# Sixteen DRAM-to-DRAM DMAs of one hybrid-mixer kernel get a fixed place in GpSimd's order

## The chip, the cores and the metric

One core of a Trainium2 chip runs the whole program in one launch. The metric is the device time of one execution in microseconds (us); lower is better. The core has TensorE (PE, with its weight loads as PEld), VectorE (DVE), ScalarE (ACT), GpSimd (POOL) and SyncE (SP), each with its own instruction order, and 16 DMA engines. All queues share those 16 engines. SP's and ACT's DMAs run on hardware queues, GpSimd's on the software queue q0.

## The reference

One layer, 512 tokens, width 2048, float32:

```python
mod = c_act @ w_ada + b_ada;  shift, scale, gate = split(mod, 3)
h = rmsnorm(x, norm_pre) * (1 + scale) + shift
q_a, f_a, v_a, z_a, v_b, z_b, g_a, g_b = split(h @ w_in, ...)
o_a = hgrn2_mixer(q_a, f_a, v_a, lb)                  # 8 heads, chunks of 64
y_a = o_a / rms(o_a) * hgrn_norm * silu(z_a)
y_b = pool_mixer(v_b, pool_w, pool_scale) * silu(z_b)
merged = sigmoid(g_a) * (y_a @ w_proj_a) + sigmoid(g_b) * (y_b @ w_proj_b)
out = merged @ w_out
x + gate * rmsnorm(out, norm_post)
```

## The kernel before

Every large product keeps float32 accuracy by splitting both operands in a high and a low part and running three matmuls. So each weight piece is loaded raw by SP (tile `..._raw`), copied to `..._hi` by ACT, and its `..._lo` is the difference, made by DVE or GpSimd. Rings of four buffers each hold the raw, the hi and the lo pieces (lines 173 to 176).

The stages, in order of time:

- **Start.** SP loads `x` (16 loads), then the rows of `w_ada` (tiles `ada`, 128 loads of 256 KB; each is 256 runs of 1 KB), mixed with pieces `A_raw`, `B_raw`, `C_raw` of `w_in` (24 loads of 512 KB, 256 runs of 2 KB each). ACT squares `x` for the norm (`junk`), DVE sums `ada` rows into `ada_acc` and `ada_sum`, `make_h` (line 295) turns a pair of row sums into two of the 16 tiles of `h` (`h_hi`, `h_lo`), and PE multiplies each piece of `w_in` with them (tile `g`). In this stage GpSimd makes `A_lo`, `B_lo`, `C_lo` and all `h_lo` (lines 317 and 653), tied in one chain by `then("POOL", ...)`. A table of planned times sets the order. The stage ends where PE begins `v_ps`.
- **Heads and pooling.** The products `q`, `v`, `vb`, `zb`, `za`; the eight heads of `hgrn` run in slices between their matmuls. `finish_a(h)` (line 572) stores a head's result to DRAM (`ya_dram`) from GpSimd's queue.
- **Gates g.** Sixteen steps (line 859) for two output tiles each. A step loads four pieces `g_raw` (512 KB, 512 runs of 1 KB each), and eleven of them also load six rows of the gate's weights, `gw` (256 KB, 128 runs of 2 KB each), which DVE sums into `gate` (lines 621 and 623). SP issues all loads in one order (`load`, line 70), each behind the one before. PE has 96 matmuls per step.
- **Projections pa, pb**, from `y` tiles which GpSimd loads back (line 891), and then the **output** product by one level of Strassen's scheme. Its B operands are sums and differences of quarters of `w_out`; four of them per half of the columns (`wsum`, eight DRAM tiles of 2 MB) are made beforehand by DMA alone.

Those sums are the matter here: 16 DMAs of 2 MB on GpSimd's queue (lines 845 to 855 list them, line 881 issues them, two per step). Eight copy a quarter of `w_out` into a `wsum` tile, four add a second quarter of `w_out`, and four add another `wsum` tile. An adding DMA waits for the copy below it and for the tile that it reads. They depend on nothing else, and the program's scheduler is free to put them anywhere in GpSimd's order that their place in the code allows. In the kernel before it has put them first. The first readers are the `wo_raw` loads of the output stage.

Of the kernel before, what the change touches and what calls it, by code (L numbers as in the profile page):

```python
# [34 lines left out]
def trunk(ctx, tc, x, c, w_ada, b_ada, norm_pre, norm_post, w_in, lower_bounds, hgrn_norm,  # L35
          pool_w, pool_scale, w_proj_a, w_proj_b, w_out, out):
    nc = tc.nc
# [15 lines left out]
    def t_s(name, dt=F32):  # L53
        return act.tile([P, S], dt, tag="s", bufs=32, name=name)

    def t_w(name, n=S, dt=F32):
        return act.tile([P, 544], dt, tag="w", bufs=10, name=name)[:, :n]
# [7 lines left out]
    def t_pg(name):  # L65
        return pg.tile([P, S], F32, tag="pg", name=name)

    last_load = [None]

    def load(dst, src):  # L70

# [10 lines left out]
    def ins_of(d):  # L82
        return getattr(d, "ins", d)
# [38 lines left out]
    def finish_heads(n):  # L122
        while steps and len(heads_done) < n:
            tick(1)
# [211 lines left out]
    def in2(name, c0):  # L336
        outs = [t_ps(f"{name}_ps0"), t_ps(f"{name}_ps1")]
        proj2(name, w_in, KT, c0, hh, hl, outs)
        return outs
# [31 lines left out]
    y_dram = [dram.tile([NH, P, S], F32, name="ya_dram"), dram.tile([NH, P, S], F32, name="yb_dram")]  # L371
# [195 lines left out]
    def gate_a(h, p):  # L567
        sz = t_w(f"sza_{h}")
        nc.scalar.activation(sz, p, AF.Silu)
        sz_a[h] = sz  # L570

    def finish_a(h):
        y = o_sb[h]
        nc.vector.scalar_tensor_tensor(y, y, vec[:, R_HN + h:R_HN + h + 1], sz_a[h], op0=ALU.mult, op1=ALU.mult)
        nc.gpsimd.dma_start(y_dram[0][h], y)

    pooled = [None] * NH

# [35 lines left out]
    def gate_rows(j, k):  # L614

        if k == 0:
            gate[j] = t_w(f"gate_{j}")
        t = t_w(f"gw_{j}_{k}")
        load(t, w_ada[k * P:(k + 1) * P, 2 * D + j * S:2 * D + (j + 1) * S])
        if k == 0:  # L620
            nc.vector.tensor_scalar(gate[j], t, c_act[:, 0:1], None, op0=ALU.mult)
        else:
            nc.vector.scalar_tensor_tensor(gate[j], t, c_act[:, k:k + 1], gate[j], op0=ALU.mult, op1=ALU.add)  # L623

    def gate_finish(j):

        acc = gate[j]
        br = t_w(f"bg_{j}")
        load(br[0:1, :], b_ada[:, 2 * D + j * S:2 * D + (j + 1) * S])
        nc.vector.tensor_add(acc[0:1, :], acc[0:1, :], br[0:1, :])  # L630
        np_b = t_w(f"npost_{j}")
        load(np_b, norm_post[:, j * S:(j + 1) * S].to_broadcast([P, S]))
        gp = t_pg(f"gate_ps_{j}")
        hi, lo = split(f"gate_{j}", acc, lambda name, dt: t_w(name, S, dt))
        matmul(gp, ones_v, hi, True, False)
        matmul(gp, ones_v, lo, False, True)
        nc.vector.scalar_tensor_tensor(acc, gp, float(P), np_b, op0=ALU.mult, op1=ALU.mult)
# [220 lines left out]
    for b, off in ((0, OFF_GA), (1, OFF_GB)):  # L858
        for m in range(0, KT, 2):
            if (b, m) == (0, ZA_AT):  # L860
                for h in range(0, NH, 2):
                    o2 = in2(f"za{h}", OFF_ZA + h * P)
                    gate_a(h, o2[0]); gate_a(h + 1, o2[1])
                    if h < 6:
                        finish_heads(h + 2)
                        finish_a(h); finish_a(h + 1)
            o2 = in2(f"g{b}_{m}", off + m * P)
            if (b, m) == (0, ZA_AT + 2):
                finish_heads(NH)
                finish_a(6); finish_a(7)  # L870

            first = ZA_AT // 2 + 2
            step = b * KT // 2 + m // 2 - first
            for i in range(max(0, step * GATE_PER), min(4 * KT, (step + 1) * GATE_PER)):
                gate_rows(i // KT, i % KT)
                if i % KT == KT - 1:
                    gate_finish(i // KT)
            if b * KT + m >= 8 and wsum_steps:
                for _ in range(2):
                    dst, src, kw = wsum_steps.pop(0)  # L880
                    nc.gpsimd.dma_start(dst, src, **kw)
            for r in range(2):
                sig[b][m + r] = t_s(f"sig{b}_{m + r}")
                nc.scalar.activation(sig[b][m + r], o2[r], AF.Sigmoid)
# [3 lines left out]
    for b in range(2):  # L888
        for k in range(NH):
            y = t_w(f"y{b}_{k}")  # L890
# [213 lines left out]
```

## Time and profile before

| | us |
|---|---|
| median of 3 runs | 1494.02 (1493.1 to 1494.7) |
| the profiled execution | 1494.7 |
| its span, first to last instruction | 1493.0 |
| PE busy | 1325.5 (89%) |
| DVE, ACT, POOL busy | 815.3, 561.0, 246.3 |
| DMA moved | 238.11 MB |

The profiled execution is 1.7 us longer than its span. The page of the profile gives totals and the chain of work that ended last. The view by stretches gives each engine's busy time, the clock that PE was granted (1.00 is 2.4 GHz, 0.50 is 1.2 GHz), the share of time the 16 DMA engines were busy, and the rate. Views in order of time show single instructions with the idle time before them and what ended it.

### The profile page before, as it was taken

How to read it: one execution, taken by the hardware profiler on the slowest of the kernel's cores; microseconds unless marked ns; L12 is line 12 of the kernel's file. 1: busy time of each engine (PE TensorE's matmuls, PEld its weight loads, DVE VectorE, ACT ScalarE, POOL GpSimd, SP SyncE). 2: the span in 40 equal slices, each digit the busy share in tenths (PEclk: the TensorE clock that was granted, in tenths of full speed). 3: DMA queues.
4: the chain of work that ended last, by engine and by line, in shares of the span. 5: the costliest groups of instructions: out<-in, count | busy, mean ns of one | idle time of the engine just before them, and what ended most of it. 6: DMA issues, size and time to landing. Idle time of an engine off the chain costs nothing.

```text
span 1493.0 us, 16400 instructions
## 1 busy us (share of the span) xinstructions
PE 1325.5 (89%) x6031; PEld 1088.9 (73%) x6031; DVE 815.3 (55%) x1336; ACT 561.0 (38%) x787; POOL 246.3 (16%) x269
## 2 busy tenths in 40 slices
PE   0230499999999999999999999999999999999996
PEld 0010377788888888887888888888888888887885
DVE  0211259754345967868768434434425455578667
ACT  3010153443353554554555422222224222245552
POOL 3100264521222232232223000000001000000010
PEclk9975699999999999999999999999999999999998
DMA  9999988933222223223233445554634333335576
GB/s 307 294 284 231 266 293 287 305 99 99 85 71 92 71 92 106 71 92 113 72 127 100 141 156 175 186 169 152 198 120 160 101 93 98 99 127 189 192 244 221
DMA packets 170232, 238.11 MB, mean 159 GB/s; under 512 B 8780, under 2 KB 120484, under 8 KB 169128
## 3 DMA queue, kind: packets, MB, share of 16 engines
q1 hardware_dynamic: 155528, 188.78, 39.4%
q0 software_dynamic: 13312, 46.14, 11.3%
q10 hardware_dynamic: 1312, 2.14, 0.4%
q8 instruction: 47, 0.77, 0.2%
q14 instruction: 33, 0.27, 0.1%
HBM read 228.64 MB, written 41.94 MB: 181 GB/s over the span
## 4 chain that ended last, share of the span: by engine, by line
PE 79%; DVE 6%; issue 4%; DMA 1%; POOL 1%; ACT 1%; DVEq 0%; ACTq 0%; POOLq 0%
PE g_ps L91 23%; PE out L91 7%; PE vb_ps L91 6%; PE za_ps L91 6%; PE v_ps L91 6%; PE pb L91 6%; PE pa L91 6%; PE g L91 5%; PE zb_ps L91 5%; PE q_ps L91 3%; PE lv L91 2%; DVE ada_acc L105 1%; PE o L91 1%; DMA ada<-in_w_ada_dram 1%; PE mix L91 1%
## 5 line engine op out<-in xcount | busy, mean ns | idle before, releaser
L91 PE MATMUL g_ps<-h_hi,g_hi 128*128 128x512 f32 x512 | 200.1, 391 | 0.0
L91 PE MATMUL g_ps<-h_hi,g_lo 128*128 128x512 f32 x512 | 199.4, 389 | 0.0
L91 PE MATMUL g_ps<-h_lo,g_hi 128*128 128x512 f32 x512 | 199.3, 389 | 0.0
L177 ACT CAST g_hi<-g_raw 128x1024 fp32r<-128x1024 f32 x64 | 67.3, 1053 | 196.3 <-PE g_ps L91 161.0
L178 DVE TENSOR_TENSOR g_lo<-g_raw,g_hi 128x1024 fp32r<-128x1024 f32 x61 | 74.5, 1222 | 108.7 <-ACT g_hi L177 107.4
L105 DVE SCALAR_TENSOR_TENSOR ada_acc<-ada,c_act,ada_acc 128x512 f32<-128x512 f32 x104 | 74.3, 751 | 92.0 <-DMA ada<-in_w_ada_dram 91.8
L91 PEld LDWEIGHTS g_ps<-h_hi,g_lo 128*128 128x128 f32 x512 | 96.1, 188 | 20.1
L91 PEld LDWEIGHTS g_ps<-h_hi,g_hi 128*128 128x128 f32 x512 | 96.1, 188 | 20.0
L91 PEld LDWEIGHTS g_ps<-h_lo,g_hi 128*128 128x128 f32 x512 | 96.1, 188 | 19.9
L178 DVE TENSOR_TENSOR wo_lo<-wo_raw,wo_hi 128x1024 fp32r<-128x1024 f32 x56 | 68.3, 1223 | 43.8 <-ACT wo_hi L177 43.8
L177 ACT CAST wo_hi<-wo_raw 128x1024 fp32r<-128x1024 f32 x56 | 59.0, 1054 | 68.2 <-PE out L91 52.9
L91 PE MATMUL g<-h_hi,A_lo 128*128 128x512 f32 x64 | 26.2, 409 | 64.9 <-POOL A_lo L105 64.9
L623 DVE SCALAR_TENSOR_TENSOR gate<-gw,c_act,gate 128x512 f32<-128x512 f32 x60 | 45.0, 751 | 44.9 <-DMA gw<-in_w_ada_dram 43.7
L91 PEld LDWEIGHTS g<-h_hi,A_lo 128*128 128x128 f32 x64 | 12.5, 196 | 68.1 <-POOL A_lo L105 65.4
L1039 POOL DMA_DIRECT2D xr<-in_x_dram x16 | 8.7, 548 | 306.2 <-PE out L91 306.2
L891 POOL DMA_DIRECT2D y<-ya_dram x8 | 4.4, 550 | 288.3 <-DMA npost<-in_norm_post_dram 231.2
L91 PE MATMUL vb_ps<-h_hi,vb_hi 128*128 128x512 f32 x128 | 51.5, 402 | 0.0
L91 PE MATMUL za_ps<-h_hi,za_hi 128*128 128x512 f32 x128 | 51.1, 399 | 0.0
L91 PE MATMUL out<-wo_lo,op_hi 128*128 128x512 f32 x128 | 49.9, 390 | 1.3 <-DVE wo_lo L178 1.3
L91 PE MATMUL zb_ps<-h_hi,zb_hi 128*128 128x512 f32 x128 | 50.9, 398 | 0.0
L91 PE MATMUL v_ps<-v_hi,h_hi 128*128 128x512 f32 x128 | 50.5, 394 | 0.0
L91 PE MATMUL vb_ps<-h_hi,vb_lo 128*128 128x512 f32 x128 | 50.1, 391 | 0.0
(343 smaller groups left out, 3394.0 us busy)
## 6 DMA issues: line engine op xcount, KB each, us to landing
ada<-in_w_ada_dram SPq DMA_DIRECT2D x128, 256.0 KB, 6.6
g_raw<-in_w_in_dram SPq DMA_DIRECT2D x64, 512.0 KB, 3.6
wsum<-in_w_out_dram POOLq DMA_DIRECT2D x12, 2048.0 KB, 40.0
gw<-in_w_ada_dram SPq DMA_DIRECT2D x64, 256.0 KB, 4.8
wo_raw<-wsum SPq DMA_DIRECT2D x32, 512.0 KB, 4.1
wo_raw<-in_w_out_dram SPq DMA_DIRECT2D x24, 512.0 KB, 4.1
wsum<-wsum POOLq DMA_DIRECT2D x4, 2048.0 KB, 37.0
v_raw<-in_w_in_dram SPq DMA_DIRECT2D x16, 512.0 KB, 3.7
```

What stands on the lines that cost most here:

```text
L91: d = nc.tensor.matmul(o, lhsT, rhs, start=start, stop=stop, skip_group_check=onto)
L105: d = f(*args, **kw)
L177: last_w[0] = ins_of(nc.scalar.copy(hi, raw))
L178: (eng or (nc.gpsimd if steps and next(turn) else nc.vector)).tensor_sub(lo, raw, hi.bitcast(F32))
L623: nc.vector.scalar_tensor_tensor(gate[j], t, c_act[:, k:k + 1], gate[j], op0=ALU.mult, op1=ALU.add)
L891: nc.gpsimd.dma_start(y, y_dram[b][k])
L1039: nc.gpsimd.dma_start(xr[t][j], x[t * P:(t + 1) * P, j * S:(j + 1) * S])
```

## The change

The 16 DMAs are issued behind the last GpSimd DMA that `finish_a` issued, and each behind the one before. `tc.issue_after` fixes an order on the engine. It adds no wait for a transfer to land.

```diff
-    last_load = [None]
+    last_load, last_pool = [None], [None]
...
     def finish_a(h):
         y = o_sb[h]
         nc.vector.scalar_tensor_tensor(y, y, vec[:, R_HN + h:R_HN + h + 1], sz_a[h], op0=ALU.mult, op1=ALU.mult)
-        nc.gpsimd.dma_start(y_dram[0][h], y)
+        last_pool[0] = ins_of(nc.gpsimd.dma_start(y_dram[0][h], y))
...
                 for _ in range(2):
                     dst, src, kw = wsum_steps.pop(0)
-                    nc.gpsimd.dma_start(dst, src, **kw)
+                    with tc.issue_after(last_pool[0]):
+                        last_pool[0] = ins_of(nc.gpsimd.dma_start(dst, src, **kw))
```

GpSimd's order at the program's start, before: the masks' last instructions, the sums (tiles `wsum_0` belong to the first half of the columns, `wsum_1` to the second), and the first difference that PE needs.

```order
L881 DMA wsum_0_4757<-wsum_0_4756 256x2048
L881 DMA wsum_1_4762<-in_w_out_dram 1024x512
L881 DMA wsum_1_4760<-wsum_1_4759 256x2048
L881 DMA wsum_1_4761<-wsum_1_4760 256x2048
L105 TENSOR_TENSOR A_lo<-A_raw,A_hi 128x1024
L105 TENSOR_TENSOR h_lo<-hf_349,h_hi 128x512
```

The same place after:

```order
L160 COPY mask_pair<-mask_pair_133 128x64
L160 COPY mask_pair<-mask_pair_138 128x64
L105 TENSOR_TENSOR A_lo<-A_raw,A_hi 128x1024
L105 TENSOR_TENSOR h_lo<-hf_349,h_hi 128x512
L105 TENSOR_TENSOR B_lo<-B_raw,B_hi 128x1024
```

All 16 sums have left the place ahead of `A_lo`; nothing but the masks stands there now.

GpSimd's order where they stand after the change, from the store of the last two heads (`ya_dram`) to the first reload of a head's result (`y_0`):

```order
L575 DMA ya_dram<-o_5386 128x512
L575 DMA ya_dram<-o_5843 128x512
L882 DMA wsum_0_4755<-in_w_out_dram 1024x512
L882 DMA wsum_0_4756<-in_w_out_dram 1024x512
L882 DMA wsum_0_4757<-in_w_out_dram 1024x512
L882 DMA wsum_0_4758<-in_w_out_dram 1024x512
L882 DMA wsum_0_4755<-in_w_out_dram 1024x512
L882 DMA wsum_0_4756<-wsum_0_4755 256x2048
L882 DMA wsum_0_4757<-wsum_0_4756 256x2048
L882 DMA wsum_0_4758<-in_w_out_dram 1024x512
```

Eight more rows of the same kind follow for `wsum_1`, and then the loads of `y`, which before stood directly behind the two stores. The order of PE, DVE, ACT and SP is the same as before but for line numbers.

## Rows read from the trace of the kernel before

**Rows 1.** The page: busy time per engine, then the chain that ended last.

```profile
PE 1325.5 (89%) x6031; PEld 1088.9 (73%) x6031; DVE 815.3 (55%) x1336; ACT 561.0 (38%) x787; POOL 246.3 (16%) x269
...
PE 79%; DVE 6%; issue 4%; DMA 1%; POOL 1%; ACT 1%; DVEq 0%; ACTq 0%; POOLq 0%
```

**Rows 2.** Stretches: length, busy us (instructions) per engine, PE's clock, DMA share, GB/s.

```profile
0.00:170.00 170.00, 25.16 (x40) 9.77 (x40) 26.66 (x48) 19.27 (x49) 25.45 (x68) 0.77 1.03 277
170.00:330.00 160.00, 153.39 (x706) 125.17 (x707) 104.33 (x155) 72.73 (x115) 75.23 (x40) 0.97 0.79 255
...
844.00:1152.00 308.00, 308.00 (x1360) 254.96 (x1359) 130.22 (x147) 85.56 (x104) 8.78 (x16) 1.00 0.52 170
```

**Rows 3.** Waits, 0 to 330 us: who waited for whom, total us, times, longest.

```profile
PE g L91 <- POOL A_lo L105: 64.9, 1, 64.9
```

**Rows 4.** POOL in order of time: start, us, instruction, idle before and releaser.

```profile
7.00 0.94 POOL L881 DMA_DIRECT2D wsum<-in_w_out_dram  x1
...
49.14 1.33 POOL L881 DMA_DIRECT2D wsum<-in_w_out_dram  x1 [22.11 <-DMA wsum<-in_w_out_dram]
...
166.85 0.88 POOL L881 DMA_DIRECT2D wsum<-wsum  x1 [34.69 <-DMA ada<-in_w_ada_dram]
167.43 2.67 POOL L105 TENSOR_TENSOR A_lo<-A_raw,A_hi 128x1024 fp32r<-128x1024 f32 x1
```

**Rows 5.** SP's issues in order of time, 0 to 175 us.

```profile
12.92 56.89 SPq L76 DMA_DIRECT2D ada<-in_w_ada_dram  x16
...
115.28 3.38 SPq L76 DMA_DIRECT2D C_raw<-in_w_in_dram  x1
118.71 40.60 SPq L76 DMA_DIRECT2D ada<-in_w_ada_dram  x8
...
170.13 0.37 SPq L76 DMA_DIRECT2D A_raw<-in_w_in_dram  x1
```

**Rows 6.** Stretches again, just after the last of the sums.

```profile
185.00:195.00 10.00, 9.91 (x56) 8.34 (x55) 4.76 (x7) 6.26 (x13) 4.43 (x3) 1.00 1.06 355
```

**Rows 7.** All engines in order of time, from the start to the released matmul.

```profile
9.48 0.61 ACT L268 ACTIVATE junk<-x 128x512 f32<-128x512 f32 x1
...
90.91 0.75 DVE L105 SCALAR_TENSOR_TENSOR ada_sum<-ada,c_act,ada_acc 128x512 f32<-128x512 f32 x1 [2.70 <-DMA ada<-in_w_ada_dram]
...
102.13 1.04 ACT L105 CAST A_hi<-A_raw 128x1024 fp32r<-128x1024 f32 x1 [48.35 <-DMA A_raw<-in_w_in_dram]
...
103.61 0.78 ACT L105 ACTIVATE h_hi<-xT,sh,g 128x512 fp32r<-128x512 f32 x1
...
170.16 0.80 PE L91 MATMUL g<-h_hi,A_lo 128*128 128x512 f32 x1 [64.92 <-POOL A_lo L105]
```

**Rows 8.** The chain that ended last, in order of time: start, us, what.

```profile
329.62 43.52 PE v_ps L91 x192
...
834.57 97.97 PE g_ps L91 x432
```

**Rows 9.** POOL: the last head's store and the first reload.

```profile
843.20 0.54 POOL L575 DMA_DIRECT2D ya_dram<-o  x1 [18.86 <-DVE o L574]
1074.96 0.55 POOL L891 DMA_DIRECT2D y<-ya_dram  x1 [231.21 <-DMA npost<-in_norm_post_dram]
```

**Rows 10.** SP and DVE in order of time, one step of the gates.

```profile
1001.11 2.88 SPq L76 DMA_DIRECT2D gw<-in_w_ada_dram  x6
...
1006.93 16.20 SPq L76 DMA_DIRECT2D g_raw<-in_w_in_dram  x4
...
1007.16 3.90 DVE L623 SCALAR_TENSOR_TENSOR gate<-gw,c_act,gate 128x512 f32<-128x512 f32 x5 [0.25 <-DMA gw<-in_w_ada_dram]
```

**Rows 11.** Waits of ACT and of SP's queue, 844 to 1152 us.

```profile
ACT g_hi L177 <- PE g_ps L91: 154.3, 45, 4.4
...
SPq L76 <- DVE g_lo L178: 210.7, 48, 6.0
```

**Rows 12.** The page's DMA queues: packets, megabytes, share of 16 engines' span.

```profile
q0 software_dynamic: 13312, 46.14, 11.3%
```

## The prediction

> **What bounds the kernel now.** I read the page first: PE is busy for 1325.5 us of 1493.0 and makes 79% of the chain that ended last [rows 1]. The view by stretches shows where it is not the bound: in the stretches shown from 170 us on PE hardly stops, but of the first 170 us it works 25 [rows 2]. There the waits name one thing: PE waits 64.9 us, once, for GpSimd's `A_lo` [rows 3]. GpSimd is not busy either. Its order in time shows the sums standing ahead of `A_lo`: the first is issued at 7.00 us, some of them wait for earlier ones to land (22.11 us at one place, 34.69 at the last), the last goes at 166.85, and `A_lo` follows at 167.43 [rows 4], though `A_hi` had been made at 102.13 [rows 7]. So the first fault is GpSimd's order. The second is in SP's order: while the sums run, its loads crawl. Sixteen `ada` loads take 56.89 us, 3.56 each, and eight later ones 40.60, 5.1 each [rows 5]. When the sums are over, the DMA engines move 355 GB/s of SP's loads alone [rows 6], 0.74 us per 256 KB. In 0 to 170 us the DMA share is already 1.03 [rows 2]: that stage is bound by DMA, and the sums are most of it.
>
> **The start, without the sums.** The 16 loads of `x` and 16 of `ada` are 32 times 0.74 us, some 24 us, issued from 1.3 us on; with 2 us to land, the last row is there at about 28. ACT squares 16 blocks of `x` from 9.48 us at 0.61 each [rows 7], to 19.3; the norm takes some 3 us of short steps, and DVE, whose order puts 11 of the 16 sums behind it, adds them at 0.75 each until about 31. From the last sum to the first matmul there lie the shift and scale, `A_hi` (1.04) and `h_hi` (0.78) [rows 7], some 4 us, and beside them `A_lo` at 2.67 [rows 4]. The matmul that was released at 170.16 [rows 7] goes at about 35. That is 135 us earlier; bounds 125 (rows landing at two thirds of that rate) and 138.
>
> From there to `v_ps` at 329.62 [rows 8] it took 159.5 us, of which PE was busy 153.4 [rows 2], the first microseconds at a lower clock (mean 0.77 over the stretch before, against 0.97). Can the stage hold this pace when it begins without the rows that the blocked kernel had already fetched? 112 `ada` loads and 22 pieces remain, 29.4 and 11.5 MB, at 355 GB/s 115 us, less than PE needs; DVE has 104.3 us of work there and some more sums, still less. I take 155 us, 4 less than before, bounds 150 to 166. **The start gains 139 us, bounds 128 to 143.** Everything between, up to the last head's store, shifts along with PE, whose order there is not touched.
>
> **The new place.** The last store goes out at 843.20 [rows 9] (I keep the clock of before for places). GpSimd then has nothing to do until it reloads `y` at 1074.96 [rows 9], 231 us later: a wait of GpSimd inside the sums holds up no one but those reloads, and the sums' issues cost nobody anything. What they bring along is the other thing: their load on the DMA engines. PE works the gates without a pause until 1152, with a DMA share of 0.52 and 170 GB/s [rows 2].
>
> How do SP's loads fare beside the sums? From 12.92 to 170.13 us SP issued 41 loads (37 `ada` and four pieces, the first and last in [rows 5]), each of 256 runs: 157.2 / 41 = 3.83 us per 256 runs. It goes by runs, not by bytes: a `C_raw` of 512 KB in 256 runs of 2 KB took SP 3.38 us, an `ada` of 256 KB in 256 runs of 1 KB 3.56 [rows 5]. A step of the gates loads four `g_raw` of 512 runs and six `gw` of 128: 2816 runs, 11 times 256, 42.1 us beside the sums. PE's 96 matmuls of the step take 97.97 / 432 * 96 = 21.8 us [rows 8]. **Beside the sums PE gets fed at 0.52 of its pace.**
>
> How long? Before, the sums lasted from 7.00 us to about 182 (the last is issued at 166.85 [rows 4], and from 185 on SP's loads have the full rate [rows 6]): 175 us. I take the same. In it PE gets food for 175 * 0.52 = 91 us; 84 are missing.
>
> What is loaded ahead pays for a part. ACT's `g_hi` waits for PE, 45 times in this stretch, and SP for DVE's `g_lo`, 48 times [rows 11]: the rings are full, four raw pieces and three split ones ahead, 7 * 5.44 = 38 us. But DVE's order also has the sums of `gw`: those that SP issues at 1001.11 are added from 1007.16 on [rows 10], and the next `g_lo` stands behind them. A late `gw` stops DVE while later `g_raw` lie there, so only the three split pieces count, 16 us. Loss: 84 - 16 = 68; with what a lower clock after PE's pauses costs, 69. Bounds: 47, if all 38 us count, to 95, if none counts and the pauses cost 10 of clock.
>
> One bound comes from another row. q0 had 11.3% of the engines' time, 169 us [rows 12]; 48 of its transfers are the 256 KB ones of `y`, `x` and the stores, at 0.74 us each 36 us, so the sums alone are worth 134 us of all 16 engines. If they lasted only that long, the loss would be 134 * 0.48 - 16 = 48.
>
> The Trainium skill ("DMA: Bandwidth & Descriptors", Anatomy of one DMA) gives 2.0 us plus the bytes over 436 GB/s for a DMA of GpSimd's queue: as an estimate by that page 6.8 us for 2 MB, 109 us for all 16, and a loss of 109 * 0.48 - 16 = 36 in place of 68. The trace speaks against it: 175 us for the same 16 beside SP's loads, 134 without them.
>
> Behind the gates nothing changes: the first reader of `wsum` is a load of the output stage, behind all the projections.
>
> **The sum.** 1494.7 (profiled execution) - 139 + 69 = 1425. The median of three is 0.7 lower than that execution, so I leave it at 1425.
>
> **The rivals.**
>
> - *Short sums:* without the exposed waits of the start they run at their own 134 us or less (by the page just named 109), loss 36 to 48: 1392 to 1404. For it: q0's share. Against: SP's loads run beside them at either place. 0.13.
> - *Hidden:* the engines have 0.48 of 308 us free, 148 us, which holds the sums' 134, and the rings cover the rest: loss 0 to 15, 1356 to 1371. Against: SP's pace in [rows 5] is what a queue gets beside the sums, not what it asks for. 0.08.
> - *A new wait at the start:* DVE's sums or late `ada` rows take `A_lo`'s place, and the gain there is about 100 us: 1455 to 1470. For it: the stage then needs DVE for over 110 of 155 us, and its rows just in time. 0.08.
> - *Slower:* SP's queue asks more at the new place than at the start, and the sums take twice as long, 350 us: the loss is 350 * 0.48 - 16 = 152, and the reloads of `y` go late too: 1508. It decides from 320 us of duration on, where the loss passes the 139 gained. For it: four of the sums wait for the one before with nothing between them. 0.04.
> - *It doesn't do what it says:* GpSimd still waits ahead of `A_lo`. The order of the instructions leaves no sum there. 0.02, 1494.
>
> **How the numbers follow.** My forecast, 1404 to 1455, has 0.65. The range of 8 in 10 reaches to the upper part of the short sums and into the weak start: 1393 to 1462. A measurement of this kernel can tell some 0.2%, 3 us, from no change. Faster 0.94, same 0.02, slower 0.04.
>
> **What the profile after would show.** Right: PE's long wait for `A_lo` gone and `v_ps` starting at 185 to 200 us; 355 GB/s from the start on; the last store of a head 139 us earlier; behind it, for 160 to 195 us, PE with pauses that DVE's `g_lo` and behind it DMAs of `gw` end, 69 us in total; no pause from there on. Wrong: `v_ps` after 210 us (the start has another bound), PE without pauses in the gates (the sums are hidden), or pauses that reach into the projections.

## The result and the profile after

The changed kernel takes 1423.28 us (median, 1418.05 to 1425.48) beside 1494.36 for the kernel before: a ratio of 0.952, 95% interval 0.9491 to 0.9549. The forecast was 1425. The profiled execution took 1424.94 us, its span 1423.2, 69.8 less than the span before.

The page of the changed kernel, answering to [rows 1] and [rows 12]: busy times, the chain that ended last by engine, the software queue.

```profile
PE 1328.0 (93%) x6031; PEld 1091.8 (77%) x6031; DVE 812.6 (57%) x1336; ACT 559.2 (39%) x787; POOL 246.3 (17%) x269
...
q0 software_dynamic: 13312, 46.14, 12.0%
...
PE 76%; DMA 14%; DVE 7%; issue 1%; SPq 1%; ACT 1%; POOL 0%; DVEq 0%; ACTq 0%
```

The work is the same; DMA now has 14% of the chain, where it had 1%. GpSimd in order of time, answering to [rows 4] and [rows 9]: the first difference, the last head's store, the sums, the first reload.

```profile
32.39 2.37 POOL L105 TENSOR_TENSOR A_lo<-A_raw,A_hi 128x1024 fp32r<-128x1024 f32 x1 [23.74 <-ACT A_hi L105]
...
706.40 0.54 POOL L575 DMA_DIRECT2D ya_dram<-o  x1 [18.86 <-DVE o L574]
706.93 3.05 POOL L882 DMA_DIRECT2D wsum<-in_w_out_dram  x4
...
813.97 1.34 POOL L882 DMA_DIRECT2D wsum<-in_w_out_dram  x1 [35.05 <-DMA wsum<-in_w_out_dram]
...
866.55 1.62 POOL L882 DMA_DIRECT2D wsum<-in_w_out_dram  x1
1005.34 0.61 POOL L892 DMA_DIRECT2D y<-ya_dram  x1 [137.18 <-DMA npost<-in_norm_post_dram]
```

`A_lo` is made at 32.39 us in place of 167.43, right behind `A_hi`; the matmul that it releases starts at 34.81 (before 170.16). GpSimd's long waits are now in the sums, where nobody waits for it. The chain in order of time, with the start of `v_ps` ([rows 8] has 329.62 for it), and pieces of it from the gates:

```profile
192.82 43.52 PE v_ps L91 x192
...
738.80 5.29 PE g_ps L91 x22
...
774.59 21.50 DMA gw<-in_w_ada_dram
796.86 1.23 DVE g_lo L178
798.13 12.49 PE g_ps L91 x46
...
812.87 29.82 DMA gw<-in_w_ada_dram
...
843.45 1.23 DVE g_lo L178
844.70 6.92 DMA g_raw<-in_w_in_dram
...
887.78 40.81 PE g_ps L91 x166
```

On this chain single loads of `gw` take 15 to 30 us. The waits of PE and of DVE behind the last store (total us, times, longest):

```profile
PE g_ps L91 <- DVE g_lo L178: 53.5, 8, 22.3
...
DVE gate L623 <- DMA gw<-in_w_ada_dram: 150.7, 29, 30.9
```

And the stretches, with the columns of [rows 2]: the start, the heads, the gates beside the sums, and the gates behind them.

```profile
35.00:190.00 155.00, 148.43 (x692) 120.99 (x692) 111.99 (x165) 71.45 (x114) 74.94 (x39) 0.98 0.85 277
193.00:706.00 513.00, 511.11 (x2485) 428.12 (x2484) 342.47 (x686) 254.54 (x348) 127.69 (x130) 1.00 0.29 91
706.00:892.00 186.00, 132.53 (x530) 105.94 (x530) 47.73 (x55) 28.52 (x34) 15.49 (x17) 0.85 1.02 277
...
912.00:1082.00 170.00, 170.00 (x752) 140.70 (x751) 71.97 (x81) 50.85 (x63) 8.86 (x16) 1.00 0.54 172
```

The table takes three marks from each trace: the start of `v_ps`, the last head's store (`ya`), and the first matmul of `pa`. The heads' column is the time from the first mark to the second, the gates' column from the second to the third. The loss in the gates is against the 308.8 us of the kernel before. Copies first, all in the start, no `gw`, `gw` not read and the first short runs were executed once each, so their times have no interval; the other times are medians.

| kernel | time | `v_ps` | `ya` | `pa` | heads | gates | loss in the gates |
|---|---|---|---|---|---|---|---|
| before | 1494 | 329.5 | 843.2 | 1152.0 | 513.7 | 308.8 | 0 |
| changed | 1423.3 | 192.7 | 706.4 | 1082.2 | 513.7 | 375.8 | 67.0 |
| copies first | 1441.2 | 243.0 | 756.7 | 1098.4 | 513.7 | 341.7 | 32.9 |
| all in the start, spaced | 1470.3 | 303.4 | 818.7 | 1127.5 | 515.3 | 308.8 | 0 |
| no `gw` | 1380.7 | 194.9 | 708.6 | 1038.7 | 513.7 | 330.1 | 21.3 |
| `gw` loaded, not read | 1409.9 | 192.2 | 706.0 | 1067.1 | 513.8 | 361.1 | 52.3 |
| short runs | 1414.1 | 194.1 | 707.8 | 1071.4 | 513.7 | 363.6 | 54.8 |
| spaced in the gates | 1384.3 | 193.5 | 707.3 | 1042.6 | 513.8 | 335.3 | 26.5 |
| the same, short runs | 1385.2 | 192.0 | 705.8 | 1040.4 | 513.8 | 334.6 | 25.8 |
| spread over the heads | 1365.3 | 191.3 | 712.5 | 1021.3 | 521.2 | 308.8 | 0 |
| the same, short runs | 1366.1 | 189.0 | 714.0 | 1022.7 | 525.0 | 308.7 | 0 |
| copies close, adds apart | 1361.6 | 191.3 | 711.3 | 1020.1 | 520.0 | 308.8 | 0 |
| copies in a block, in the heads | 1362.6 | 193.0 | 709.6 | 1018.3 | 516.6 | 308.7 | 0 |

Start -136.8, gates +67.0: net 69.8, the difference of the two spans.

### The profile page after: what moved, and what is told of

Read it like the earlier page. It is cut to its first block, busy times and chain, and to the rows that moved or that the text cites. A ratio compares the mean times of both kernels' runs of the same rounds, so it can differ in the third digit from the quotient of the medians.

```text
span 1423.2 us, 16399 instructions
## 1 busy us (share of the span) xinstructions
PE 1328.0 (93%) x6031; PEld 1091.8 (77%) x6031; DVE 812.6 (57%) x1336; ACT 559.2 (39%) x787; POOL 246.3 (17%) x269
## 3 DMA queue, kind: packets, MB, share of 16 engines
q0 software_dynamic: 13312, 46.14, 12.0%
## 4 chain that ended last, share of the span: by engine, by line
PE 76%; DMA 14%; DVE 7%; issue 1%; SPq 1%; ACT 1%; POOL 0%; DVEq 0%; ACTq 0%
PE g_ps L91 18%; PE out L91 8%; DMA gw<-in_w_ada_dram 8%; PE vb_ps L91 6%; PE za_ps L91 6%; PE v_ps L91 6%; PE pb L91 6%; PE pa L91 6%; PE g L91 5%; PE zb_ps L91 5%; DMA ada<-in_w_ada_dram 4%; PE q_ps L91 3%; PE lv L91 2%; DMA g_raw<-in_w_in_dram 1%; SPq L76 1%
## 5 line engine op out<-in xcount | busy, mean ns | idle before, releaser
L91 PE MATMUL g_ps<-h_hi,g_lo 128*128 128x512 f32 x512 | 205.3, 401 | 53.5 <-DVE g_lo L178 53.5
L91 PE MATMUL g_ps<-h_hi,g_hi 128*128 128x512 f32 x512 | 204.5, 399 | 0.0
L91 PE MATMUL g_ps<-h_lo,g_hi 128*128 128x512 f32 x512 | 203.2, 397 | 0.0
L91 PEld LDWEIGHTS g_ps<-h_hi,g_hi 128*128 128x128 f32 x512 | 99.0, 193 | 20.6
L91 PE MATMUL za_ps<-h_hi,za_lo 128*128 128x512 f32 x128 | 50.0, 391 | 0.0
L91 PE MATMUL vb_ps<-h_lo,vb_hi 128*128 128x512 f32 x128 | 50.0, 390 | 0.0
L91 PE MATMUL zb_ps<-h_hi,zb_lo 128*128 128x512 f32 x128 | 49.9, 390 | 0.0
```

The source lines that it names most:

```text
L91: d = nc.tensor.matmul(o, lhsT, rhs, start=start, stop=stop, skip_group_check=onto)
```

## The experiments

Two theories stood against each other for each half of the change. At the start: did GpSimd's blocked order make it late, or the sums' load on the DMA engines? In the gates: what makes PE wait there, and could it be avoided? The cuts of the edits show where a sum is issued; where the building of the list of sums moves with it, that part is left out.

**Copies first.** The eight copies go back to the program's start, the eight adds stay behind the last store.

```diff
-                    with tc.issue_after(last_pool[0]):
-                        last_pool[0] = ins_of(nc.gpsimd.dma_start(dst, src, **kw))
+                    if kw:
+                        with tc.issue_after(last_pool[0]):
+                            last_pool[0] = ins_of(nc.gpsimd.dma_start(dst, src, **kw))
+                    else:
+                        nc.gpsimd.dma_start(dst, src)
```

> The eight copies go back to the program's start, ahead of A_lo; the eight adding DMAs stay behind the last head's store. Copies wait for nothing, so GpSimd is free for A_lo at about 15 us. Theory (shared DMA engines): the start is late by the DMA load alone. The copies last some 80 to 90 us there, 32 loads of x and ada take as long, and v_ps starts at 240 to 265 us in place of 192.8. The adds alone last some 115 us beside the gates and cost 30 to 40 us there in place of 67. Together 1445 to 1465 us. Rival (GpSimd's order): only the waits on GpSimd ahead of A_lo cost time at the start; v_ps starts at 195 to 200 us, and the total is 1390 to 1400 us.

Measured 1441.2 us; `v_ps` at 243.0, loss in the gates 32.9. The copies wait for nothing, so GpSimd was not blocked: ahead of `A_lo` it waits for ACT's `A_hi`.

```profile
81.45 2.35 POOL L105 TENSOR_TENSOR A_lo<-A_raw,A_hi 128x1024 fp32r<-128x1024 f32 x1 [66.59 <-ACT A_hi L105]
```

And yet the start came 50 us later than in the changed kernel, so the rival falls. The total lies 4 us below the range given, since start and loss both came out in the lower halves of theirs.

**All sums in the start, none that waits ahead of the first difference.** The copies at the program's start, the adds one by one in GpSimd's chain of the start stage.

```diff
         chains[engine] = ins_of(d)
+        if engine == "POOL":
+            pieces[0] += 1
+            if pieces[0] >= ADDS_FROM and pieces[0] % 3 == 0 and wsum_list:
+                dst, src2, kw = wsum_list.pop(0)
+                with tc.issue_after(chains[engine]):
+                    chains[engine] = ins_of(nc.gpsimd.dma_start(dst, src2, **kw))
```

> All 16 sums at the start again, but not as a block ahead of GpSimd's first difference: the eight copies at the program's start, the eight adds one by one between GpSimd's differences of the start stage, every third one from the twelfth on. Theory A (the sums' load on the DMA engines made the start late, GpSimd's order only put that in one place): first matmul of g at 80 to 90 us as with the copies alone, v_ps at 295 to 325, nearly as late as before the change, no loss in the gates, total 1458 to 1490. Theory B (GpSimd's blocked order made it late): v_ps at 240 to 255 as with the copies alone, total 1403 to 1420.

Measured 1470.3 us, `v_ps` at 303.4. Waits of GpSimd, ACT and DVE in its first 303 us (total us, times, longest), and the stretch itself:

```profile
POOL A_lo L107 <- ACT A_hi L107: 103.5, 4, 67.4
...
ACT A_hi L107 <- DMA A_raw<-in_w_in_dram: 73.1, 5, 27.4
...
DVE ada_acc L107 <- DMA ada<-in_w_ada_dram: 117.0, 32, 25.7
...
0.00:303.00 303.00, 184.20 (x742) 139.97 (x743) 131.25 (x201) 91.20 (x163) 99.94 (x106) 0.90 0.99 289
```

Now it is GpSimd that waits for ACT, and ACT and DVE for SP's loads; none of GpSimd's waits there is for a sum, and the DMA engines are busy for 0.99 of the time. Theory A holds: with the order mended and the sums still in the stage, `v_ps` comes 26 us earlier than before the change; the other 111 us come only when the sums leave the stage.

**What the late `gw` cost.** First 60 of the 64 `gw` loads with their sums are left out of the changed kernel, then the loads stay and only 60 of DVE's sums are left out.

```diff
+        if k > 0:
+            return
```

```diff
-        else:
-            nc.vector.scalar_tensor_tensor(gate[j], t, c_act[:, k:k + 1], gate[j], op0=ALU.mult, op1=ALU.add)
```

> The changed kernel with 60 of the 64 rows of the gate's weights left out, their loads and their sums on DVE (the gate vector is then incomplete). Theory (SP's loads are late by runs, and the late gw rows stop DVE ahead of g_lo): a step needs 2048 runs, 30.7 us beside the sums against 21.8 of PE, and with no gw sum in DVE's order all the 38 us of pieces ahead count: the loss in the gates falls from 67 us to 0 to 15, total 1358 to 1373. Rival (the sums disturb something else: PE's clock, GpSimd and DVE on one port, memory as such): the pauses stay, above 1400.

> The changed kernel with the same gw loads, but 60 of the 64 sums on DVE that read them are left out (the gate vector is then incomplete). SP's queue has the same runs to move; only DVE no longer waits for gw ahead of g_lo. Theory: the missing food is the same 84 us, but 38 us of pieces ahead count in place of 16, so the loss is 45 to 55 in place of 67: total 1403 to 1413. Rival a (all of the loss is DVE's wait for gw): total 1358 to 1370. Rival b (the pieces ahead play no part): 1425.

Measured 1380.7 us, 8 above the theory's range, and 1409.9, within it. PE's waits behind the last store, without `gw` (the first two lines) and then with `gw` not read:

```profile
PE g_ps L91 <- DVE g_lo L178: 8.7, 5, 6.6
PE g_ps L91 <- ACT g_hi L177: 4.7, 3, 1.9
```

```profile
PE g_ps L91 <- ACT g_hi L177: 25.9, 5, 13.9
PE g_ps L91 <- DVE g_lo L178: 12.1, 5, 6.7
```

So of the 67.0 us, 15 go when DVE's order no longer stops at a late `gw`, as expected (45 to 55 left). That kernel also spares DVE 60 sums and SP its waits until DVE has read a `gw`, 11.4 us in the changed kernel; no run takes these apart. Another 31 go with the loads of `gw`. The 21 that are left without `gw` are more than the 0 to 15 expected: 13.4 us of waits, and the rest is matmuls that took longer. PE did 719 matmuls in 170.62 busy us of this stretch at a granted clock of 0.96:

```profile
708.00:892.00 184.00, 170.62 (x719) 137.50 (x718) 37.18 (x36) 36.09 (x44) 15.49 (x17) 0.96 1.01 263
```

At [rows 8]'s 97.97 / 432 = 0.227 us each they are worth 163.1, so 7.5 us are slower matmuls.

**Short runs.** All sums are asked for in runs of 1 KB; the copies and the adds from `w_out` and from `wsum` had 2, 2 and 8 KB.

```diff
-            wsum_steps += [(dst, first, {}), (dst, second, {"accum_op": ALU.add, "max_dma_last_dim": 8192})]
+            wsum_steps += [(dst, first, {"max_dma_last_dim": 1024}), (dst, second, {"accum_op": ALU.add, "max_dma_last_dim": 1024})]
```

> The changed kernel with all 16 sums cut in runs of 1 KB, copies too; same place, same bytes. Theory (the DMA engines take turns by runs, so a short run of the sums holds SP's next one up for less time): SP gets more food per us beside the sums, the sums last 215 to 330 us, the loss in the gates, from the last head's store to the first projection, falls from 67 to 20 to 50 us, total 1378 to 1408. If only the adds are cut in the end, the loss is 30 to 45. Rival (the engines share by bytes or by time, whatever the size of a run): the loss stays at 60 to 75, total 1418 to 1432.

Measured 1414.1 us, loss 54.8: between the two theories. The queue's packets tell that only the adds were cut (13312 before, 11264 more now, which is what the eight adds make at 1 KB):

```profile
q0 software_dynamic: 24576, 46.14, 13.5%
```

Something is gained, less than by the theory of turns. Both halves of that theory's account are seen: in 186 us behind the last store SP issued 24 pieces `g_raw` and 36 `gw` in place of 21 and 31, and the last sum (issued at 902.36 us, 38.3 us to landing) was there at 940.7 us in place of 897.2, so the sums stood beside SP's loads for longer.

```profile
g_raw<-in_w_in_dram SPq DMA_DIRECT2D x24, 512.0 KB, 11.8
...
gw<-in_w_ada_dram SPq DMA_DIRECT2D x36, 256.0 KB, 17.0
...
902.36 4.67 POOL L882 DMA_DIRECT2D wsum<-in_w_out_dram  x1
```

**Spread over the heads.** Each second difference that GpSimd makes in the heads' stage is followed by one sum, copies first, then the adds of the two halves in turn.

```diff
-        (eng or (nc.gpsimd if steps and next(turn) else nc.vector)).tensor_sub(lo, raw, hi.bitcast(F32))
+        e = eng or (nc.gpsimd if steps and next(turn) else nc.vector)
+        d = ins_of(e.tensor_sub(lo, raw, hi.bitcast(F32)))
+        if e is nc.gpsimd and wsum_list:
+            pieces[0] += 1
+            if pieces[0] % SUM_EVERY == 0:
+                dst, src2, kw = wsum_list.pop(0)
+                with tc.issue_after(d):
+                    nc.gpsimd.dma_start(dst, src2, **kw)
```

> The sums are issued one at a time between GpSimd's lo pieces of the heads and pooling stage, some 22 us apart, the eight copies first and then the adds of the two halves in turn. Theory: a sum of 2 MB lasts 10 to 14 us beside SP's loads, the stage's loads then run at half pace for that long and at full pace for the rest of the 22 us, and 38 us of pieces ahead cover it: no loss anywhere, the start stays at 192.8 us and the gates go without a pause: 1355 to 1365 us. Rival (the same DMA work costs PE the same wherever it lies beside its loads): about 1425. A second rival: an adding DMA's wait on GpSimd holds up the lo pieces behind it, 1370 to 1400.

Measured 1365.3 us (1360.82 to 1370.14), a ratio of 0.9142 (0.9111 to 0.9173) to the kernel before, 0.3 us above the theory's range: the gates lose nothing, the heads 7.5 us, where no loss was expected.

**The same with short runs of the adds, and with the adds further apart.** The second has the copies behind every difference and the adds behind every third.

```diff
-            if pieces[0] % SUM_EVERY == 0:
+            if len(wsum_list) > 8 or pieces[0] % SUM_EVERY == 0:
```

> The kernel with the sums spread over the heads' stage, its eight adds cut in runs of 1 KB in place of 8 KB. Theory (turns by runs; the two pauses of PE near 469 and 558 us stand beside adds with 8 KB runs): the pauses beside the adds go, v_ps to the last head's store takes 513 to 517 us in place of 521, total 1356 to 1363. Rival (the pauses come from the bytes): 521 us again, total 1361 to 1370.

> The same spread, 8 KB runs kept, the copies behind every difference of GpSimd and the adds behind every third. Theory (the pauses come from adds that are issued 16 to 25 us apart and each last about as long): with 30 to 40 us between adds the pauses go, total 1356 to 1363. Rival (copies at 10 to 14 us apart now starve SP in the v stage): new pauses between 230 and 340 us, total 1366 to 1385.

With short runs 1366.1 us (0.9153, 0.9131 to 0.9176), heads 525.0 us: no gain, so the theory of turns falls here as a forecast. The adds themselves took longer, 22.4 and 21.6 us (median, from `w_out` and from `wsum`) in place of 19.3 and 15.1. With the adds apart 1361.6 us (0.9108, 0.9093 to 0.9124), inside its range. Its interval and that of the first spread overlap a little, and the heads' stage took 520.0 us in place of 521.2: crowding the copies did no harm, but that the distance of the adds brings a gain isn't shown.

**Is it the place or the spacing?** The spread kernels changed both. So one kernel spaces the sums within the gates (GpSimd splits every third piece of `g` and issues a sum behind it), and one puts the copies as a block into the heads' stage (the adds apart as above).

```diff
-        e = eng or (nc.gpsimd if steps and next(turn) else nc.vector)
+        pieces[0] += gates[0]
+        e = eng or (nc.gpsimd if (steps and next(turn)) or (gates[0] and wsum_list and pieces[0] % SUM_EVERY == 1) else nc.vector)
```

```diff
-                dst, src2, kw = wsum_list.pop(0)
+                for _ in range(8 if len(wsum_list) > 8 else 1):
+                    dst, src2, kw = wsum_list.pop(0)
```

> The sums stay in the gates' stage, where the change put them, but are issued one at a time: every third piece of g is split by GpSimd in place of VectorE, and one sum follows it, some 16 us apart; copies first, adds of the two halves in turn. Theory (a row of sums without gaps starves SP; with gaps SP catches up at its full pace): while a sum runs (12 us) SP loads 3.1 of the 256-run units, in the 4.4 us of gap another 5.9, together 9.0 where PE needs 8.3, so the loss from the last head's store to the first projection is 0 to 20 us, total 1357 to 1378. Rival (the place decides: the gates' own loads leave too little of the DMA engines, however the sums are spaced): loss 40 to 70, total 1397 to 1430.

> The eight copies in one block at the first difference of GpSimd in the heads' stage, the eight adds behind every third difference. Theory (what counts is what the stage asks of SP: there one piece of 512 runs in some 6 us and no gw rows, against 7.7 us for it beside the sums, so 0.78 of PE's pace; a block of 85 us misses 19 us, and the rings hold 38): the block is hidden, v_ps to the last head's store takes 513 to 519 us, total 1356 to 1364. Rival (a block costs wherever it stands, as the eight copies cost 50 us at the start): 20 to 40 us lost there, total 1378 to 1400.

The block in the heads is hidden: 1362.6 us (0.9121, 0.9107 to 0.9134), heads 516.6 us, theory held. Its stretch with the block, from 190 to 300 us, has PE busy throughout beside a DMA share of 0.75:

```profile
190.00:300.00 110.00, 110.00 (x517) 91.79 (x516) 48.27 (x99) 48.90 (x63) 26.66 (x26) 1.00 0.75 246
```

Spaced in the gates the sums cost 26.5 us, 1384.3 in all (0.927, 0.9239 to 0.9301): between the theory's range and the rival's. Its GpSimd also takes 16 differences out of DVE's order, where a late `gw` would hold them up, so not all of what is gained on the block need be the spacing; no run takes the two apart. Its two stretches, first the copies, then the adds:

```profile
706.00:846.00 140.00, 139.98 (x617) 115.57 (x616) 58.94 (x60) 34.89 (x42) 25.59 (x17) 1.00 0.82 270
846.00:1042.00 196.00, 177.26 (x750) 145.01 (x749) 65.67 (x73) 49.66 (x63) 36.20 (x32) 0.94 0.94 244
```

And the DMA issues from 846 us on (KB each, median us to landing), after a line for the copies before that:

```profile
wsum<-in_w_out_dram POOLq DMA_DIRECT2D x8, 2048.0 KB, 12.6
```

```profile
wsum<-in_w_out_dram POOLq DMA_DIRECT2D x4, 2048.0 KB, 20.8
wsum<-wsum POOLq DMA_DIRECT2D x4, 2048.0 KB, 15.4
```

Copies of 12.6 us, 16 us apart, cost PE nothing. The expectation took 12 us for every sum, but adds take 15 to 21 us, and two of them at times come close together; the loss lies in their stretch, with PE's longest pause (11.1 us, until 927.76) behind the two adds issued at 900.11 and 908.18. Whether the adds' 8 KB runs are to blame was asked with one more kernel, the same with runs of 1 KB:

```diff
-            wsum_steps += [(dst, first, {}), (dst, second, {"accum_op": ALU.add, "max_dma_last_dim": 8192})]
+            wsum_steps += [(dst, first, {}), (dst, second, {"accum_op": ALU.add, "max_dma_last_dim": 1024})]
```

> The kernel with the sums spaced in the gates, its eight adds cut in runs of 1 KB in place of 8 KB. In the one with 8 KB runs the copies (718 to 850 us) cost PE nothing and the adds (from 850 us on) cost 26.6 us. Theory (an 8 KB run holds SP's next run up for longer, so the adds with long runs are what starves SP): 3 to 15 us are left, total 1361 to 1373. Rival (an add costs because it reads and writes more bytes than a copy, whatever its runs): 22 to 32 us lost as with 8 KB runs, total 1380 to 1390.

Measured 1385.2 us (0.9274, 0.9256 to 0.9292), loss 25.8: the rival held. Long runs are not what makes an add dear; with short ones the adds took 26.2 and 30.8 us in place of 20.8 and 15.4, for the same loss.

## Why the prediction was right, and where it was not

**The start, right in size.** 136.8 us gained of 139 forecast (bounds 128 to 143). The released matmul came at 34.81 (forecast 35), the stage from there to `v_ps` took 158 us in place of 155: DVE's sums waited only 8.4 us in it for `ada` rows, and PE, busy for 148.43 of 155 us, could not have saved more than the rest. The rival of a new wait at the start fell. The rate of 355 GB/s that was to hold "from the start on" did so only ahead of that matmul (354 from 20 to 30 us); from 35 to 190 us it was 277.

**But its first reason was wrong.** The prediction calls GpSimd's order "the first fault" and the DMA load a second. The kernel with all sums in the start shows the order to be worth 26 us there and the load 111. PE's one long wait for `A_lo` [rows 3] was the place where the lateness showed: in that kernel and in the one with the copies first GpSimd is free, and it waits 67 us for `A_hi`, and ACT and DVE for `A_raw` and the `ada` rows. (The last wait of GpSimd that the prediction takes for a sum's, 34.69 us, is put down to an `ada` load in [rows 4]; the sum issued there at 131.27 us landed 35.1 us later, so the prediction's reading stands.) The same section read the DMA share of 1.03 and concluded "that stage is bound by DMA, and the sums are most of it"; that was the reason. The size came out right because the working of the start went by SP's rate without the sums, not by the length of GpSimd's waits.

**The gates, right in sum by two errors that cancel.** Loss 67.0 us, forecast 69. (Two slips of the working change nothing: 84 + 10 is 94 and not 95, and 169 - 36 is 133 and not 134.)

- *How long the sums last:* from 706.93 to 897.2 (the sum issued at 866.55 lands 30.6 us later), 190 us; the stretch from 892 on is the first without a pause of PE. Forecast 175.
- *What SP gets beside them:* forecast one unit of 256 runs per 3.83 us. The DMA issues from 706 to 892 us count what it got:

```profile
g_raw<-in_w_in_dram SPq DMA_DIRECT2D x21, 512.0 KB, 10.9
...
gw<-in_w_ada_dram SPq DMA_DIRECT2D x31, 256.0 KB, 20.2
```

  21 * 2 + 31 / 2 = 57.5 units in 186 us, 3.2 us each. PE wants 11 units in 21.8 us, 94 in 186, so the feed was 0.61 and not 0.52, and 72 us were missing (forecast 84). By bytes the rate differs even more from that of the start, so neither count carries over exactly; why SP fared better here was not tried.
- *What the rings cover:* 21 pieces are food for 504 matmuls, PE did 530, so 26 of them, 6 us, came from what lay ahead. Forecast 16, by the argument that a late `gw` stops DVE while later pieces of `g_raw` lie there. The chain's rows from 774.59 to 843.45 show that very order. The kernel that does not read `gw` shows what it costs: from 22 pieces in the same stretch PE did 614 matmuls, 86 or 20 us of them from what lay ahead, and it has 15 us less loss.

```profile
g_raw<-in_w_in_dram SPq DMA_DIRECT2D x22, 512.0 KB, 17.0
...
706.00:892.00 186.00, 151.01 (x614) 120.31 (x613) 30.82 (x29) 33.37 (x41) 15.45 (x17) 0.89 1.05 291
```

- *The clock:* forecast 1 us, bound 10, from no row. In 706 to 892 PE did 530 matmuls, worth 120.2 us at 0.227, in 132.53 busy us at a mean granted clock of 0.85, between the levels of 1.2 and 2.4 GHz: 12.3 us more. Eight pauses of up to 22.3 us are not one; the row to read was [rows 2], where the start's pauses already gave a mean of 0.77. But slower matmuls are not yet lost time where PE would have waited for its next piece in any case. From the first pause on the chain has PE in three pieces, 234 matmuls in 58.59 us, 5.5 more than at 0.227; the rest of it is loads of `gw` and `g_raw`, DVE and SP. So the clock cost some 5.5 us at most by that chain, and no run sets it apart.

So up to 892 us 72 - 6 stands where 84 - 16 was forecast: too little food by 12 us, too much cover by 10. In PE's own time the 67.0 us are 53.5 of pauses and 13.5 of slower matmuls, where 68 and 1 were forecast.

**Nothing behind the gates changed**, as forecast: no sum was still running at `pa`, and from 912 us on PE has no pause.

**The rivals.** Short sums: no, 190 us; by the formula of the Trainium skill ("DMA: Bandwidth & Descriptors", Anatomy of one DMA) a sum takes 6.8 us as an estimate. No sum here landed in that; the copies spaced in the gates took 12.6. Hidden: not in one block in the gates. In the heads' stage it is nearly what happens, and SP's pace beside the sums says why: in 706 to 892 us it was 21 pieces of 512 KB and 31 of 256 KB, 103 GB/s; without the sums the heads' stage moves 91, the gates 172. Slower: the sums did not stretch beyond 190 us.

**What the prediction did not ask** is whether the new place was a good one. Of the three stages the start had a DMA share of 0.85 without the sums, the gates 0.54 and the heads 0.29. The heads' stage takes the same sums for 3 to 11 us, some 60 us less than the gates: the kernels with copies close and adds apart, and with the block in the heads, take 1361.6 and 1362.6 us and are the fastest here. Their intervals overlap.

## What to carry to other kernels

A long wait for an engine whose own queue is stuck on DMAs says where the lateness shows, not what it costs: before moving the instructions, ask what the waiting engine would wait for next, and how busy the DMA engines are in that stage. Background transfers belong in the stage where the loads that PE needs ask least of the DMA engines, ahead of the stage that reads them; here even a block of copies was hidden there, and in the busier stage spacing hid the copies but not the adds. When a block does land in a busy stage, count the feed and what the rings really cover (pieces behind a late side load count less), and read on the chain how much of a lower clock is lost time.

## What was not expected of the hardware

- Eight pauses of PE, 53.5 us in all, came with a mean granted clock of 0.85 in the stretch and 13.5 us of slower matmuls, of which the chain shows 5.5; without `gw`, 13.4 us of pauses came with 0.96 and 7.5 us.
- Cutting the adds from 2 and 8 KB to 1 KB runs changed nothing in the time where the sums are spaced (1384.3 and 1385.2 us; 1365.3 and 1366.1), though the adds took up to twice as long. In the block it gave 12 us in the gates, in a single comparison; why only there stays open. The Trainium skill ("DMA: Bandwidth & Descriptors", Queues, rings and completion order) has each DMA engine alternate between queues packet by packet. If short runs make short packets, SP's loads should come through sooner and the adds last longer: the longer adds are seen, a gain in the spaced kernels is not.
- An add of 2 MB from DRAM to DRAM takes 15 to 21 us beside SP's loads in the gates, a copy of 2 MB 12.6.
